# 64-byte pads between operand buffers of a two-block transformer kernel, and two weight sums that trade places

## Chip, cores, metric

The kernel runs on one core of one Trainium2 chip. The metric is device time of one execution in microseconds (us), the median over runs. Everything below is read from one profiled execution of the kernel before, and from the programs as they are built: the addresses of buffers and the order of instructions are in the built program, no time is.

## What is computed

Two transformer blocks on 512 tokens of width 1024, in float32. The reference, cut to its frame:

```python
def first_block(x, ...):
    h = rms_norm(x, norm1_w[l])
    cols = split_cols(h @ w_in[l], IN_SIZES)
    y = concatenate([short_conv_mixer(...), nsa_mixer(...), mla_mixer(...), stick_breaking_mixer(...)])
    x = x + rms_norm(y, out_norm_w) @ w_out[l]
    h2 = rms_norm(x, norm2_w[l])
    return x + square(relu(h2 @ ffn_w1[l])) @ ffn_w2[l]

def second_block(x, ...):
    h = rmsnorm(x, norm_mix_pre[l])
    proj = h @ w_in[l]
    ...
    x = x + rmsnorm(merged @ w_out[l], norm_mix_post[l])
    h = rmsnorm(x, norm_ffn_pre[l])
    f = (silu(h @ ffn_w_gate[l]) * (h @ ffn_w_up[l])) @ ffn_w_down[l]
    return x + rmsnorm(f, norm_ffn_post[l])
```

Nearly all of the work is dense products of a [512, 1024] activation (or a wider hidden one) with weight matrices.

## The kernel before

**Split products.** Every operand of a dense product is held as two float32r tiles, `hi` and `lo`, whose sum is the float32 value (`K.split`, L284 to 291: ScalarE writes `hi`, VectorE writes `lo`). A product is then three matmuls into the same PSUM bank (`K.mm3`, L317 to 321):

```python
nc.tensor.matmul(out, a[0], b[0], start=start, stop=False)
nc.tensor.matmul(out, a[0], b[1], start=False, stop=False)
nc.tensor.matmul(out, a[1], b[0], start=False, stop=stop)
```

`a` is the stationary operand (128 columns, loaded into the array by a weight load of its own for every matmul), `b` the moving one. Lines L319, L320 and L321 of the profile are these three. While matmul k streams its moving operand, the weight load of matmul k+1 reads the next stationary operand.

**Who moves and who stands.** In `tok_tile` (L486) the activation stands and the weights move, 256 columns at a time (240 or so in a few). In `fm_tile` (L503) the weights stand and the activation moves, 512 columns at a time, or 256 where only half of the tokens are there yet. In `down_tile` (L630, the second matrices of both feed-forward parts) the hidden activation stands and the weights move, 256 columns (512 for the first group of the second block). `Fast` (L510 to 607, the first matrices of both feed-forward parts) forms seven products of quarters in place of eight; weight quarters or sums of them (`a11 a12 a22 s1 s2 s3 s4`) stand, quarters of x or sums of them (`t1` to `t4`) move, 256 columns each, four mm3 a product.

**Buffers.** Tiles come from pools that are laid out in each partition one behind the other in the order in which they are opened: `cst`, `big` (one pair of activation operands), `wraw`, `wsp` (four slots each of `whi` and `wlo`, 4096 bytes), `sm` (small columns), then the pools of a phase. Almost every tile is a multiple of 128 bytes long, so the position of a buffer within 128 bytes is set by the few short tiles before it. With "half 0" for a start at a multiple of 128 and "half 64" for one that is 64 bytes behind it, the built program has: `whi`, `wlo` 0; the pair in `big` (`xh`, `xl` of both mixers, and in each feed-forward part the sums t1 to t4) 0; the first block's feed-forward operand x 64; `brh`, `brl` (the second block's branch operand, later its feed-forward operand x) 64; `hh`, `hl` (hidden activation) 64; `sah/sal` (a11, a12), `ssh/ssl` (s1, s2), `sdh/sdl` (a22) 64. The sums s3 and s4 lie in the quarter of x that no product reads, so in half 64 as well.

**Order.** The feed-forward parts interleave steps of `Fast.unit` (L577) and of the down product by a table (`merge`, PACE1 and PACE2); a scheduler then interleaves further. Everything that TensorE reads has been split by ScalarE and VectorE before.

Of the kernel before, what the change touches and what calls it, by code (L numbers as in the profile page):

```python
# [18 lines left out]
P = 128  # L19
S = 512  # L20
NT = S // P
# [32 lines left out]
# --------------------------------------------------------------------------  # L54
# host side: layout only, and constants that depend on shapes alone
# --------------------------------------------------------------------------
def _fm(w):
    """[K, n*128] -> [n, 128, K]: panels of 128 columns, all row tiles."""
    k, n = w.shape
    return np.ascontiguousarray(w.reshape(k // P, P, n // P, P).transpose(2, 1, 0, 3)).reshape(n // P, P, k)  # L60


def _kp(w, kt=4, width=256):
    """[K, n*width] -> [n * K/(128*kt), 128, kt*width]: panels of kt row tiles, the row tiles inner."""
    k, n = w.shape
    return np.ascontiguousarray(
        w.reshape(k // (P * kt), kt, P, n // width, width).transpose(3, 0, 2, 1, 4)
    ).reshape(-1, P, kt * width)
# [36 lines left out]
def prep(inp):  # L105
# [38 lines left out]
    # ---- block 2  # L144
# [74 lines left out]
# --------------------------------------------------------------------------  # L219
# device side  # L220
# --------------------------------------------------------------------------
class K:
    """Shared pools, constants and small building blocks."""

    def __init__(self, tc, a, ctx, dbg):
        self.tc, self.nc, self.a, self.dbg = tc, tc.nc, a, dbg or {}
        e = ctx.enter_context
        self.cst = e(tc.tile_pool(name="cst", bufs=1))
        self.big = e(tc.tile_pool(name="big", bufs=1))
        self.wraw = e(tc.tile_pool(name="wraw", bufs=2))  # L230
        self.wsp = e(tc.tile_pool(name="wsp", bufs=4))
        self.sm = e(tc.tile_pool(name="sm", bufs=2))
        self.dram = e(tc.tile_pool(name="dram", bufs=1, space=DRAM))
        self.ps = e(tc.tile_pool(name="ps", bufs=1, space=PSUM))
        self.n = self.flip = self.turn = self.turn2 = 0
# [6 lines left out]
        self.cols = self.cst.tile([P, a["cols"].shape[1]], F32, name="cols")  # L242

# [12 lines left out]
    def wide(self):  # L256
        """A bank for a phase of dense products alone, which has six of the eight."""
        t = WIDE[self.turn % len(WIDE)]
        self.turn += 1
        return self.psum(t)  # L260
# [13 lines left out]
    def late_dma(self, dst, src):  # L274
        """A constant of a later part: its load stays out of the way of the first ones."""
        with self.tc.issue_after(self.late.ins):
            self.nc.gpsimd.dma_start(dst, src)
# [5 lines left out]
    # hi + lo = src * scale exactly, each with 12 significant bits  # L283
# [9 lines left out]
    def copy(self, dst, src):  # L293
        """A copy out of PSUM, on ScalarE and VectorE in turn."""
# [6 lines left out]
    def weights(self, src, n, ahead=None, slot=None, parts=1):  # L301
        """One panel [128, n] from DRAM, split; slot: where it stays, if not among the others."""
# [20 lines left out]
    def spread(self, pool, out, r):  # L323
        """out[p, 128 t + i] = r[i, t]"""
# [6 lines left out]
    def mm2(self, out, a, n, hi, lo, start, stop):  # L331
        """a: hi and lo side by side, hi in the first n; out: their products one under the other."""
        steps = [(out[:n], a[:, :n], lo)]
        # the first and the last of all go to all of out
# [10 lines left out]
    def exp_ln(self, after):  # L345
        """The table set with Exp and Ln, once the activation `after` has been issued."""
# [4 lines left out]
    def rstd(self, ss, n, cnt, eps=EPS, after=None):  # L351
        """[128, n] sums of squares -> 1/sqrt(sum/cnt + eps), with one Newton step."""
# [14 lines left out]
    def junk(self):  # L367
        """Where the squares go of which only the sum is used."""
        return self.sm.tile([P, D], BF16, tag="njk", bufs=1, name=self.nm("njk"))

    def norm_table(self, pool, j, bufs=1):
        """The weight of a norm over the model width, on every partition."""
# [4 lines left out]
    def to_operand(self, op, h, t, keep=False):  # L377
        """Token-major h [128, 1024] of token tile t -> transposed, split into op; keep: also in place of h."""
# [12 lines left out]
    def norm_in(self, op, x, wt, h, t, keep=False):  # L391
        """RMS norm of token-major x [128, 1024], times wt, into the operand op; h: scratch."""
# [13 lines left out]
class Emission:  # L406
    """The parts of a phase, emitted step by step in the order of a plan."""
# [24 lines left out]
def operand(k, pool, tag):  # L432
    """A pair (hi, lo) of a whole feature-major activation."""
# [6 lines left out]
def softmax_unit(k, p, ps, bias, scale, init, acc, ssum):  # L440
    """ps: scores -> p = exp(logits - max); acc = -max, ssum = sum."""
# [5 lines left out]
def transposed(k, dst, p, n):  # L447
    """p [128 q, n keys] -> its 128-blocks transposed, [128 keys, n] in dst."""
# [7 lines left out]
def y_norm(k, y, W=256):  # L456
    """RMS-normalise token-major y [128, NT, 256] in place (weight excluded)."""
# [10 lines left out]
def heads_to_T(k, y, g, yT, w):  # L468
    """token-major y [128, NT, 256] -> transposed, weighted, split into tiles 2g, 2g + 1 of yT."""
# [9 lines left out]
def tok_tile(k, xop, t, panels, n, ps, order=range(KT)):  # L479
    """ps[128 tok, n] = x[tok tile t] @ W, W in two panels of four row tiles."""  # L480
# [15 lines left out]
def fm_tile(k, xop, w, ps, c0=0, c1=S):  # L496
    """ps[128 out features, tokens c0..c1] = W^T x, W the panel of these features."""
# [5 lines left out]
class Fast:  # L503
    """
    Products of a weight matrix with the activation x in Winograd's form of Strassen's algorithm: of the
    quarters A (the weights: output tiles by halves of the rows) and B (x: halves of the rows by halves of
    the tokens), seven products of sums in float32 instead of eight.
    """

    def __init__(self, k, x, full):  # L510
        """x: hi and lo; full(t): x of the token tile t in float32, which the sums take the place of."""
        self.k, self.x, self.full = k, x, full

    def quarter(self, i, j):
        """B of rows half i, tokens half j."""
        return [z[:, 4 * i : 4 * i + 4, 256 * j : 256 * j + 256] for z in self.x]

    def sums(self, j):
        """The sums of quarters of x, for the token tiles j and j + 2."""
# [8 lines left out]
    def split(self, t):  # L528
        """The sums, split, into t."""
# [8 lines left out]
    def weights(self, src0, src1):  # L538
        """Quarters and sums of quarters of two panels, split: by name, hi and lo, in four row tiles."""
# [3 lines left out]
        with k.tc.high_priority(AHEAD):  # L543
# [7 lines left out]
            def slot(tag, n, names):  # L551
                t = [B.tile([P, n], F32R, tag=tag + z, name=k.nm(tag + z)) for z in "hl"]
# [3 lines left out]

            k.split(*slot("sa", 1024, ("a11", "a12")), r0)
            k.split(*slot("sd", 512, ("a22",)), a22)
            slot("ss", 1024, ("s1", "s2"))
            # the quarter of x that no product takes makes room for two sums  # L560
            for i, nm in enumerate(("s3", "s4")):
                w[nm] = [z[:, 2 * i : 2 * i + 2, :].rearrange("p a (b m) -> p a b m", m=P) for z in self.quarter(0, 1)]
# [9 lines left out]
    def product(self, out, l, r):  # L572
        """out[128, 256 tokens] = quarter l of the weights, transposed, times quarter r of x."""
# [4 lines left out]
    def unit(self, src0, src1, u):  # L578
        """u[128, 2, 512] = the two output tiles of the panels src0, src1, in a step for each product."""
# [34 lines left out]
def merge(plan, **gens):  # L614
    """The steps of several generators in the order of a plan, then what is left of them."""
# [7 lines left out]
def down_tile(k, hs, t, w, kt, n, ps):  # L623
    """ps[128 tok, n] = h[tok tile t] @ W over kt tiles of hidden features."""
# [14 lines left out]
def first_block(k, xd):  # L639
    nc, tc, a = k.nc, k.tc, k.a  # L640
    xin = a["x"].rearrange("(t p) d -> p t d", p=P)
    with ExitStack() as ctx:
# [18 lines left out]
        # the norm's factor, by token: in columns, and on every partition  # L661
# [29 lines left out]
    # ---- output projection, residual; feed-forward: relu(h2 @ W1)^2 @ W2  # L691
    with ExitStack() as ctx:
# [5 lines left out]
        xop = operand(k, B, "x")  # L698

# [3 lines left out]
        def spare(z):  # L703
# [4 lines left out]
            + [spare(z) for z in ("sa", "ss")]  # L708
        )
        full = [B.tile([P, 2, D], F32, tag=z, bufs=2, name=k.nm("xf")) for z in ("hh", "hl")]  # L710
        fast = Fast(k, xop, lambda t: full[t // 2][:, t % 2, :])
        fast.pool = B
# [60 lines left out]
        for g in range(8):  # L773
            hs = pieces()
            if g == 0:
                # the first half of the tokens: the others are still on their way
# [1221 lines left out]
```

## Time and profile before

| | |
|---|---|
| runs shown | 1768.1, 1769.1, 1775.0 us; median 1769.1 |
| span of the profiled execution, first to last instruction | 1768.9 us |
| TensorE matmul busy | 1736.7 us (98%), 12,443 instructions |
| TensorE weight load busy | 1613.1 us (91%), 12,443 |
| VectorE, ScalarE, GpSimd busy | 1178.8 (67%), 878.6 (50%), 99.1 us (6%) |
| granted TensorE clock, mean | 0.993 |

No time of the profiled execution apart from its span is shown; the span is 0.2 us under the median. Matmuls are pipelined, so the busy time of one (about 280 ns for 256 columns) is longer than the distance from its start to the next one's start. That distance, called pitch below, is what sums to the span. A table of stretches counts every matmul that overlaps a stretch, so the pitch there is (length of the stretch + the time one lasts) / count.

### The profile page before, as it was taken

The numbers are of one execution on the slowest core, as the hardware profiler recorded it, in microseconds if no ns is written. First come the engines' busy times: TensorE is split into PE (matmuls) and PEld (weight loads), VectorE is DVE, ScalarE is ACT, GpSimd is POOL, SyncE is SP. The second block draws the span as 40 slices with busy tenths as digits, with TensorE's granted clock in tenths as the row PEclk, the third lists the DMA queues.
The fourth block names the chain that finished last, engine by engine and source line by source line (L and its number), as shares of the span: only waits on it lengthen the run. The fifth ranks groups of instructions, "written<-read, shape, count | busy, mean of one in ns | idle before, by whom it ended". The sixth has DMA issues, their size and how long they took to land. (4 is left out here: it accounts for less than half of the span.)

```text
span 1768.9 us, 30605 instructions
## 1 busy us (share of the span) xinstructions
PE 1736.7 (98%) x12443; PEld 1613.1 (91%) x12443; DVE 1178.8 (67%) x2194; ACT 878.6 (50%) x1625; POOL 99.1 (6%) x130
## 2 busy tenths in 40 slices
PE   8999999999999999999999999999999999999997
PEld 8888689999999998898889988889988989999997
DVE  5867855877777776987344453345436589888886
ACT  6654754553444444677324452435553565444442
POOL 0101002000000020000000000000000400000002
PEclk9999989999999999999999999999999999999999
DMA  6422104222233332121223222222235223233233
GB/s 218 159 84 71 44 1 179 84 96 97 96 107 108 104 115 97 55 90 60 84 96 108 84 69 91 97 94 72 92 100 173 90 98 118 96 108 110 94 108 108
DMA packets 50797, 174.92 MB, mean 99 GB/s; under 512 B 6075, under 2 KB 6619, under 8 KB 50656
## 3 DMA queue, kind: packets, MB, share of 16 engines
q1 hardware_dynamic: 48384, 165.38, 27.9%
q0 software_dynamic: 2272, 7.59, 1.4%
q8 instruction: 98, 1.61, 0.4%
q14 instruction: 43, 0.35, 0.1%
HBM read 166.63 MB, written 6.31 MB: 98 GB/s over the span
## 5 line engine op out<-in xcount | busy, mean ns | idle before, releaser
L288 DVE TENSOR_TENSOR wlo<-raw,whi 128x1024 fp32r<-128x1024 f32 (+2 forms) x209 | 253.5, 1214 | 188.5 <-ACT whi L287 183.0
L287 ACT ACTIVATE whi<-raw 128x1024 fp32r<-128x1024 f32 (+2 forms) x209 | 217.7, 1042 | 297.7 <-PE mm L320 167.1
L319 PE MATMUL mm<-whi,xh 128*128 128x256 f32 (+1 forms) x720 | 205.7, 287 | 7.4 <-ACT whi L287 6.6
L319 PE MATMUL mm<-xh,whi 128*128 128x512 f32 (+1 forms) x544 | 207.5, 382 | 0.6 <-DVE swv L288 0.6
L321 PE MATMUL mm<-xh,wlo 128*128 128x512 f32 (+1 forms) x544 | 206.9, 380 | 0.0
L320 PE MATMUL mm<-xl,whi 128*128 128x512 f32 (+1 forms) x544 | 206.6, 380 | 0.0
L320 PE MATMUL mm<-wlo,xh 128*128 128x256 f32 (+1 forms) x720 | 205.1, 285 | 0.0
L321 PE MATMUL mm<-whi,xl 128*128 128x256 f32 (+1 forms) x720 | 204.6, 285 | 0.0
L319 PEld LDWEIGHTS mm<-whi,xh 128*128 128x128 f32 x720 | 138.0, 192 | 9.1 <-ACT whi L287 6.6
L320 PEld LDWEIGHTS mm<-wlo,xh 128*128 128x128 f32 x720 | 138.1, 192 | 1.7 <-issue 0.9
L321 PEld LDWEIGHTS mm<-whi,xl 128*128 128x128 f32 x720 | 137.9, 192 | 1.1 <-issue 0.9
L319 PE MATMUL mm<-whi,hh 128*128 128x256 f32 (+1 forms) x428 | 119.2, 280 | 0.4 <-ACT hh L287 0.4
L320 PE MATMUL mm<-wlo,hh 128*128 128x256 f32 (+1 forms) x428 | 119.5, 279 | 0.0
L321 PE MATMUL mm<-whi,hl 128*128 128x256 f32 (+1 forms) x428 | 119.3, 279 | 0.0
L319 PEld LDWEIGHTS mm<-xh,whi 128*128 128x128 f32 x544 | 102.3, 188 | 18.4 <-DVE swv L288 0.8
L321 PEld LDWEIGHTS mm<-xh,wlo 128*128 128x128 f32 x544 | 102.4, 188 | 18.0
L320 PEld LDWEIGHTS mm<-xl,whi 128*128 128x128 f32 x544 | 102.4, 188 | 17.3
L319 PE MATMUL mm<-brh,whi 128*128 128x512 f32 (+1 forms) x224 | 84.9, 380 | 0.2 <-ACT brh L287 0.2
L320 PE MATMUL mm<-brl,whi 128*128 128x512 f32 (+1 forms) x224 | 84.4, 377 | 0.7 <-DVE brl L288 0.7
L321 PE MATMUL mm<-brh,wlo 128*128 128x512 f32 (+1 forms) x224 | 84.8, 379 | 0.0
L319 PEld LDWEIGHTS mm<-whi,hh 128*128 128x128 f32 x428 | 80.4, 188 | 0.8 <-ACT hh L287 0.6
L320 PEld LDWEIGHTS mm<-wlo,hh 128*128 128x128 f32 x428 | 80.5, 188 | 0.2
(797 smaller groups left out, 5026.3 us busy)
## 6 DMA issues: line engine op xcount, KB each, us to landing
raw<-in_f_dram SPq DMA_DIRECT2D x50, 512.0 KB, 3.5
raw<-in_gates_dram SPq DMA_DIRECT2D x24, 512.0 KB, 3.4
raw<-in_wb_dram SPq DMA_DIRECT2D x24, 512.0 KB, 3.5
raw<-in_fd_dram SPq DMA_DIRECT2D x22, 512.0 KB, 4.1
raw<-in_wo_dram SPq DMA_DIRECT2D x16, 512.0 KB, 4.1
raw<-in_rvg_dram SPq DMA_DIRECT2D x16, 512.0 KB, 3.4
raw<-in_gvg_dram SPq DMA_DIRECT2D x16, 512.0 KB, 3.4
sraw<-in_f_dram SPq DMA_DIRECT2D x14, 512.0 KB, 3.8
```

Of the source, the lines that this page charges most:

```text
L287: nc.scalar.activation(hi, src, AF.Copy)
L288: nc.vector.tensor_tensor(lo, src, hi.bitcast(F32), ALU.subtract)
L319: nc.tensor.matmul(out, a[0], b[0], start=start, stop=False)
L320: nc.tensor.matmul(out, a[0], b[1], start=False, stop=False)
L321: nc.tensor.matmul(out, a[1], b[0], start=False, stop=stop)
```

## The change

Seven tiles of 64 bytes (`pad`, 128 partitions x 16 floats) are put between other tiles, each with a memset on GpSimd. In `Fast.weights` a22 takes the place of s4 in the unused quarter of x, s4 takes a22's place in `sd`, and `ss` may come from a pool of its own that follows the phase's pool. The diff without the lines that only drop comments:

```diff
@@ class K, __init__
         self.wraw = e(tc.tile_pool(name="wraw", bufs=2))
+        self.shift(e(tc.tile_pool(name="wpad", bufs=1)))
         self.wsp = e(tc.tile_pool(name="wsp", bufs=4))
         self.sm = e(tc.tile_pool(name="sm", bufs=2))
+        self.shift(e(tc.tile_pool(name="spad", bufs=1)))
...
+    def shift(self, pool):
+        self.nc.gpsimd.memset(pool.tile([P, 16], F32, name=self.nm("pad")), 0.0)
@@ class Fast, weights
             def slot(tag, n, names):
-                t = [B.tile([P, n], F32R, tag=tag + z, name=k.nm(tag + z)) for z in "hl"]
+                pool = self.spool if tag == "ss" else B
+                t = [pool.tile([P, n], F32R, tag=tag + z, name=k.nm(tag + z)) for z in "hl"]
...
+            for i, nm in enumerate(("a22", "s3")):
+                w[nm] = [z[:, 2 * i : 2 * i + 2, :].rearrange("p a (b m) -> p a b m", m=P) for z in self.quarter(0, 1)]
             k.split(*slot("sa", 1024, ("a11", "a12")), r0)
-            k.split(*slot("sd", 512, ("a22",)), a22)
+            k.split(*w["a22"], a22.rearrange("p (a b m) -> p a b m", a=2, m=P))
             slot("ss", 1024, ("s1", "s2"))
-            for i, nm in enumerate(("s3", "s4")):
-                w[nm] = [z[:, 2 * i : 2 * i + 2, :].rearrange("p a (b m) -> p a b m", m=P) for z in self.quarter(0, 1)]
+            slot("sd", 512, ("s4",))
@@ first_block, feed-forward
         xop = operand(k, B, "x")
+        k.shift(B)
...
-            + [spare(z) for z in ("sa", "ss")]
+            + [spare("sa"), k.shift(B) or spare("ss")]
         )
+        k.shift(B)
         full = [B.tile([P, 2, D], F32, tag=z, bufs=2, name=k.nm("xf")) for z in ("hh", "hl")]
-        fast.pool = B
+        fast.pool = fast.spool = B
@@ second_block, feed-forward
-        fast.pool = B
+        fast.pool, fast.spool = B, ctx.enter_context(tc.tile_pool(name="ffn2s", bufs=1))
         wt = k.norm_table(B, 5)
         fo = B.tile([P, NT, D], F32, name="fo")
+        k.shift(B)
+        k.shift(fast.spool)
```

In the built program `whi`, `wlo` go from half 0 to half 64, `hh`, `hl`, `sah/sal`, `sdh/sdl` from 64 to 0; `ssh/ssl`, the operands x of the feed-forward parts and the pair in `big` stay. Counted over all float32r matmuls in their order, by the half in which the moving operand starts and the half in which the stationary operand of the next matmul starts (some 200 with another position are left out):

| columns, halves (moving, next stationary) | before | with the change |
|---|---|---|
| 256, (0, 0) | 2,819 | 710 |
| 256, (64, 64) | 1,319 | 536 |
| 256, (0, 64) | 4,030 | 1,610 |
| 256, (64, 0) | 566 | 5,879 |
| 512, (0, 0) | 1,419 | 76 |
| 512, (64, 64) | 0 | 570 |
| 512, (0, 64) | 58 | 1,343 |
| 512, (64, 0) | 568 | 56 |

With the change, about 300 of the equal pairs of 256 columns stand alone, at a switch between two kinds of product.

Instructions keep their number and, on TensorE, their place; names change. TensorE in the second block's feed-forward part, behind a piece of the down product, where a product of the unit in work begins (`mm_17737`; its operands are the moving `brh/brl`, and s4). Before:

```order
L320 MATMUL mm_17937<-wlo_17767,hh_16921 128x256
L319 MATMUL mm_17737<-brh_13910 128x256
L320 MATMUL mm_17737<-brl_13911,brh_13910 128x256
L321 MATMUL mm_17737<-brh_13910,brl_13911 128x256
L319 MATMUL mm_17737<-brh_13910 128x256
```

And with the change:

```order
L327 MATMUL mm_17960<-wlo_17796,hh_16944 128x256
L326 MATMUL mm_17760<-brh_13926,sdh_17693 128x256
L327 MATMUL mm_17760<-brl_13927,sdh_17693 128x256
L328 MATMUL mm_17760<-brh_13926,sdl_17694 128x256
L326 MATMUL mm_17760<-brh_13926,sdh_17693 128x256
```

The matmuls are the same; s4 is read from `sd` where it was read from `br`. ScalarE in the same part, the `hi` halves of one unit's weights (`sd` was a22, the `br` rows s3 and s4; the other rows of the stretch belong to the down product). Before:

```order
L287 ACTIVATE sdh_16372<-sraw_16365 128x512
...
L287 ACTIVATE ssh_16376<-sraw_16365 128x512
L287 ACTIVATE sah_16368<-raw_16364 128x1024
L287 ACTIVATE brh_13910<-sraw_16365 128x2x256
L287 ACTIVATE ssh_16376<-sraw_16365 128x512
L1950 ACTIVATE u_16189<-u_16189 128x1024
L287 ACTIVATE brh_13910<-raw_16364 128x2x256
```

And with the change (`sd` is s4, the `br` rows a22 and s3):

```order
L294 ACTIVATE brh_13926<-sraw_16388 128x2x256
...
L294 ACTIVATE ssh_16397<-sraw_16388 128x512
L294 ACTIVATE sah_16391<-raw_16387 128x1024
L294 ACTIVATE brh_13926<-sraw_16388 128x2x256
L294 ACTIVATE ssh_16397<-sraw_16388 128x512
L1963 ACTIVATE u_16212<-u_16212 128x1024
L294 ACTIVATE sdh_16399<-raw_16387 128x512
```

The six pieces have the same sizes and stand in the same order.

## Rows read from the trace of the kernel before

**Rows 1.** The page's busy times by engine.

```profile
PE 1736.7 (98%) x12443; PEld 1613.1 (91%) x12443; DVE 1178.8 (67%) x2194; ACT 878.6 (50%) x1625; POOL 99.1 (6%) x130
```

**Rows 2.** Stages: stretch, length, busy (instructions) by engine, PEclk, DMA share, GB/s.

```profile
357.60:626.40 268.80, 268.80 (x2343) 268.79 (x2342) 204.77 (x319) 125.65 (x162) 0.00 (x0) 1.00 0.31 103
...
1437.60:1731.50 293.90, 292.67 (x2479) 289.98 (x2478) 248.26 (x409) 131.91 (x188) 0.00 (x0) 1.00 0.34 112
1731.50:1768.90 37.40, 24.72 (x218) 24.52 (x216) 24.09 (x44) 12.09 (x31) 12.12 (x10) 0.90 0.28 85
```

**Rows 3.** The same table, stretches of 256-column matmuls of one kind alone.

```profile
674.00:687.00 13.00, 13.00 (x110) 13.00 (x110) 6.12 (x8) 4.20 (x6) 0.00 (x0) 1.00 0.19 58
...
606.00:608.60 2.60, 2.60 (x24) 2.60 (x23) 2.44 (x4) 2.10 (x3) 0.00 (x0) 1.00 0.00 2
549.50:563.00 13.50, 13.50 (x121) 13.50 (x120) 8.12 (x15) 2.82 (x4) 0.00 (x0) 1.00 0.47 152
...
336.00:357.00 21.00, 21.00 (x181) 21.00 (x180) 12.00 (x17) 4.87 (x7) 0.00 (x0) 1.00 0.32 101
321.20:334.80 13.60, 13.60 (x122) 13.60 (x122) 13.22 (x20) 10.19 (x16) 0.00 (x0) 1.00 0.22 72
1428.50:1437.50 9.00, 9.00 (x79) 9.00 (x78) 7.25 (x10) 6.34 (x8) 0.58 (x1) 1.00 0.21 66
```

**Rows 4.** TensorE in order of time, feed-forward of block one: start, length, instruction.

```profile
374.52 0.28 PE L319 MATMUL mm<-xh,sah 128*128 128x256 f32 x1
...
375.94 0.29 PE L319 MATMUL mm<-xh,ssh 128*128 128x256 f32 x1
...
377.32 0.28 PE L319 MATMUL mm<-xh,sah 128*128 128x256 f32 x1
```

**Rows 5.** TensorE in order of time, two breaks by transposes (L385).

```profile
318.01 0.60 PE L385 MATMUL tp<-ident,xf 128*128 128x128 f32 x4
...
318.57 0.28 PE L321 MATMUL mm<-xh,wlo 128*128 128x256 f32 x1
...
319.98 0.28 PE L321 MATMUL mm<-xh,wlo 128*128 128x256 f32 x1
...
320.45 0.60 PE L385 MATMUL tp<-ident,xf 128*128 128x128 f32 x4
```

**Rows 6.** TensorE in order of time, where both operands change halves.

```profile
335.06 0.28 PE L321 MATMUL av<-xh,wlo 128*128 128x256 f32 x1
335.18 0.28 PE L319 MATMUL mm<-whi,hh 128*128 128x256 f32 x1
335.30 0.28 PE L320 MATMUL mm<-wlo,hh 128*128 128x256 f32 x1
335.42 0.28 PE L321 MATMUL mm<-whi,hl 128*128 128x256 f32 x1
```

**Rows 7.** TensorE in order of time, 512 columns: first and last of three runs.

```profile
665.33 0.39 PE L321 MATMUL mm<-xh,wlo 128*128 128x512 f32 x1
...
673.49 0.39 PE L321 MATMUL mm<-xh,wlo 128*128 128x512 f32 x1
...
884.15 0.39 PE L319 MATMUL mm<-brh,whi 128*128 128x512 f32 x1
...
888.73 0.39 PE L321 MATMUL mm<-brh,wlo 128*128 128x512 f32 x1
...
1098.82 0.40 PE L321 MATMUL mm<-brh,wlo 128*128 128x512 f32 x1
...
1103.72 0.40 PE L321 MATMUL mm<-brh,wlo 128*128 128x512 f32 x1
```

**Rows 8.** Groups by line and shape: count, then busy us, mean ns, idle before.

```profile
L319 PE MATMUL mm<-whi,xh 128*128 128x256 f32 x688 | 196.8, 287 | 7.4 <-ACT whi L287 6.6 <-ACT xh L290 0.7
...
L320 PE MATMUL mm<-wlo,hh 128*128 128x256 f32 x420 | 116.3, 277 | 0.0
```

More of the change, by code (lines that the diff above doesn't have):

```diff
@@ L226, in __init__ @@
         self.tc, self.nc, self.a, self.dbg = tc, tc.nc, a, dbg or {}
+        self.n = self.flip = self.turn = self.turn2 = 0
         e = ctx.enter_context
@@ L230, in __init__ @@
         self.wraw = e(tc.tile_pool(name="wraw", bufs=2))
+        self.shift(e(tc.tile_pool(name="wpad", bufs=1)))
         self.wsp = e(tc.tile_pool(name="wsp", bufs=4))
         self.sm = e(tc.tile_pool(name="sm", bufs=2))
+        self.shift(e(tc.tile_pool(name="spad", bufs=1)))
         self.dram = e(tc.tile_pool(name="dram", bufs=1, space=DRAM))
         self.ps = e(tc.tile_pool(name="ps", bufs=1, space=PSUM))
-        self.n = self.flip = self.turn = self.turn2 = 0
         self.mixed = False
```

## The prediction

> **What bounds the kernel now.** I read the busy line of the page first [rows 1]: matmuls cover 98% of the span, VectorE 67%, ScalarE 50%, GpSimd 6%. The stage table then shows the two feed-forward loops, 268.80 and 293.90 us, in which TensorE idles for 0.00 and 1.23 us at a full granted clock [rows 2]. So TensorE's own pace sets the time, and the change leaves its instructions and their order alone. What is left to it is the pitch of one matmul against the next, and that is not one number. Stretches of the same work, three matmuls of 256 columns a product, differ [rows 3]; with the 0.28 us of the last one added to each length:
>
> - moving operand and next stationary operand in equal halves: 13.28/110 = 120.7 ns for (0, 0) at 674 us, 2.88/24 = 120.0 for (64, 64) at 606 us. One matmul more or less at the edges shifts the first by 1%, so I take 120.0 for both.
> - opposite halves: 13.78/121 = 113.9 for (0, 64) at 549 us and 13.88/122 = 113.8 for (64, 0) at 321 us, but 21.28/181 = 117.6 for (0, 64) at 336 us and 9.28/79 = 117.5 for (64, 0) at 1,428 us. All six stretches have a granted clock of 1.00, which is the upper of the two levels (2.4 GHz), and TensorE idles in none.
>
> So opposite halves have two paces, called **fast** (113.8) and **middle** (117.6) here, and both sign pairs show both. At 512 columns the order is turned round [rows 7]: equal halves (0, 0) take (673.49 - 665.33)/36 = 226.7 ns, opposite ones (884.15 to 888.73 over 20) 229.0 or (1,098.82 to 1,103.72 over 21) 233.3. The groups agree with the first finding from another side: the mean of one matmul is 287 ns where whi and xh, both in half 0, meet, and 277 where wlo and hh, in opposite halves, do [rows 8].
>
> **What picks the pace** is how a run begins. Behind the first of two transposes, twelve matmuls from 318.57 to 319.98 us go at 117.5 ns, behind the second, with the same operands, the next 122 go fast [rows 5, 3]. At 335.18 us moving and stationary operand both change halves with one equal pair between, and the run behind it, entered from a fast one, stays at 117.6 for its whole stretch [rows 6, 3]. Inside the feed-forward loop, by contrast, twelve equal pairs (1.42/12 = 118.3 ns) stand between two fast runs of (0, 64), and the next twelve are at 115.0 with the settling in it [rows 4]: a long run of equal pairs seems to hand over in the fast pace, a single one does not always.
>
> **The change, part by part.** Counts are of the built programs; prices are [rows 3] unless said.
>
> *Token-tile products of the mixers and both projections:* some 2,230 matmuls of 256 columns (whi, wlo moving, half 0 to 64) go from equal to (64, 0). All fast they give 2,230 x 6.2 = -13.8 us, all middle 2,230 x 2.4 = -5.4. They are broken up by transposes and element-wise waits, and behind a break both paces occur [rows 5], so I take the middle between them, **-9.6**.
>
> *Feed-forward loops:* 4,767 matmuls of 256 columns. Their time now is 268.80 + 293.90 - 1.23 idle - 11.0 (48 matmuls of 512 columns by [rows 7]) = 550.5 us [rows 2], or 115.5 each: a quarter (1,226) equal, the rest mostly fast. With the change nearly all are opposite, but half of them (64, 0), and where the work passes between kinds of product both operands flip, which leaves a lone equal pair, as at 335.18 us [rows 6]. All fast: 4,767 x 113.8 = 542.5. All middle: 560.6. Some 300 lone pairs at 120 in place of either add 1.9 or 0.7. So -6.1 to +10.8. The nearest rows for the entry are split (rows 4 fast, rows 6 middle), so I take half and half: 551.5 + 1.3, **+2.3**. This is the term on which the sign hangs.
>
> *512 columns:* 1,343 pairs go from (0, 0) to (0, 64), 570 from (64, 0) to (64, 64). With 226.7 for equal and 229.0 for opposite [rows 7]: +3.1 - 1.3 = **+1.8**. If the new opposite ones are at 233.3 it is +8.9 - 1.3 = +7.6; if the ones removed are half at 233.3 and the new ones at 229.0, +0.5.
>
> *Losers:* the same pads make equal pairs of some that are opposite now: 174 at 305 to 328 us, where the stretch at 321 us is fast, 185 at 1,405 to 1,431 us, where the one at 1,428 us is middle, and 135 of the first output projection, which I take as middle too. 174 x 6.2 + 320 x 2.4 = **+1.8**; all of them fast now, it would be +3.1.
>
> *Last stage,* from 1,731.5 us: 24.72 us for 218 matmuls, 113.4 each, all (0, 64) and fast [rows 2]. They become (64, 0): nothing if fast, 209 x 3.8 = 0.8 if middle; I take **+0.4**.
>
> *Pads and swapped sums:* seven memsets on GpSimd, which works for 99.1 us in 130 instructions, 0.76 each [rows 1]: 5.3 us on an engine with nothing to do in either loop [rows 2], and no one reads a pad. If that cover were gone, a memset would hold up TensorE only where it delayed a tile's first writer. a22 and s4 have the same size, the same writers and the same place in ScalarE's order, and the pools keep their number of buffers, so no wait is added: **0** for both.
>
> Sum: -9.6 + 2.3 + 1.8 + 1.8 + 0.4 = -3.3, so 1,765.6 from the profiled span of 1,768.9, and 0.2 more against the median of the runs, 1,769.1. I predict **1,765.5**. A measurement of this kernel can tell about 0.5%, 8.8 us, from no change; by that bound this is no change.
>
> The row that speaks for the change is the 120.0 of equal against 113.8 of opposite halves at the same clock and with no idle time [rows 3]. The Trainium skill, "TensorE: Matmul & The Clock Gate", in its step-by-step part, step 1, says against it: "Loading the next tile's weights doesn't steal SBUF read bandwidth from the running matmul." By that sentence the halves would not matter and the sum would be 0; the trace disagrees, by 6.2 ns in 120.
>
> **Rivals.**
>
> *1. Every opposite pair runs fast.* For it: in the loops nearly all opposite pairs are fast now (115.5 on average with a quarter equal [rows 2], 113.9 at 549 us [rows 3]). Against it: rows 5 and 6. It gives -13.8 - 6.1 + 1.8 + 1.8 + 0 - 0.8 (the 191 at 336 us become fast too) = -17.1, so 1,752; with the 512 columns at their lower end, 1,750.7.
>
> *2. The middle pace takes the loops, and it is slower.* Today the loops owe their fast pace to long runs of equal pairs that reset it [rows 4]; the change removes these and puts a flip of both operands in their place, the one form of entry that rows 6 show going into the middle pace. Then -5.4 + 10.8 + 1.8 + 1.8 + 0.8 = +9.8, so 1,779, and with 512 columns at 233.3 (+7.6 for +1.8) 1,784.7. From all fast to all middle the time rises by 26.9 us; so it is slower by over 8.8 us once less than 4% of the pairs are fast with 512 columns at 229.0, or less than a quarter at 233.3.
>
> *3. Halves are not the cause,* but go along with it: which product, which buffer. For it: only one place in the trace shows the same product in both paces [rows 5]. Against it: all equal stretches are at 120, four places with other operands and stages are not [rows 3]. It gives 1,769. The sentence of the Trainium skill above stands on this side.
>
> **How the numbers follow.** Rows 4 and 6 are one against one for the loops; forecast (a mixture) 0.47, rival 1 0.33, rival 2 0.15, rival 3 0.05. Forecast and rival 3 lie within 0.5%, rival 1 beyond it on the fast side, rival 2 at 1,779 and over on the slow side: faster 0.33, same 0.52, slower 0.15. The range goes from just under rival 1 with 512 columns at their lower end, 1,749, to rival 2 with 512 columns about a third of the way to their upper end, 1,781.
>
> **What would show it.** Right: pure stretches of whi against xh fall from 120 to 113.8 or 117.6, with the mean of that group falling from 287 [rows 8]; 512-column runs of xh at 229 or more; the lengths of the two loops add up to about 565. Rival 1 shows loops of 557 together, rival 2 of 573. Wrong altogether would be equal pairs at less than 120 or opposite ones at 120, a third pace, or idle time of TensorE in the loops, which would mean that something other than the pads moved.

## The result, and the profile after

The change makes the kernel slower: 1,786.0 us median (1,782.6 to 1,789.0, 4 runs) against 1,768.6 (1,766.1 to 1,775.0, 4 runs). The ratio, of the means, is 1.0092, with a 95% interval of 1.007 to 1.0114. The profiled execution spans 1,783.8 us. The prediction was 1,765.5, no change, in a range of 1,749 to 1,781; it was wrong. Two executions of some 4,406 us, one of run f2 below and one of the kernel before, are in no ratio of this text.

The busy line of the page, with the change, answers to [rows 1]:

```profile
PE 1752.6 (98%) x12443; PEld 1622.1 (91%) x12443; DVE 1176.9 (66%) x2194; ACT 879.8 (49%) x1625; POOL 98.2 (6%) x137
```

The same 12,443 matmuls take 15.9 us more, and no other engine moves by more than 2 us. The stage table with the change has the two feed-forward loops, the last stage (the columns are those of [rows 2]), and, second, 4,095 matmuls of the second block's mixers:

```profile
362.60:635.90 273.30, 273.30 (x2343) 273.30 (x2342) 205.15 (x319) 125.91 (x163) 0.00 (x0) 1.00 0.30 101
683.80:1375.10 691.30, 690.51 (x4095) 604.30 (x4094) 373.42 (x726) 342.10 (x647) 17.26 (x43) 1.00 0.28 91
1449.40:1746.20 296.80, 295.25 (x2480) 292.80 (x2479) 248.41 (x409) 132.09 (x188) 0.00 (x0) 1.00 0.34 110
1746.20:1783.80 37.60, 25.56 (x218) 25.35 (x216) 24.14 (x44) 12.09 (x31) 12.14 (x10) 0.89 0.27 85
```

The mixers' stage of the kernel before:

```profile
673.90:1362.80 688.90, 688.12 (x4096) 608.12 (x4096) 373.30 (x726) 341.71 (x646) 17.89 (x43) 1.00 0.28 91
```

Loops +4.5 and +2.9 us, mixers +2.4, last stage's matmuls +0.8, at a granted clock that is the same to 0.01. TensorE idles for 0.3 us more in the second loop (1.55 for 1.23) and for no more than 0.01 us more in the other three stages. The pitch did it. The matmuls of the six stretches of [rows 3], with the change:

```profile
683.90:696.60 12.70, 12.70 (x110) 12.70 (x109) 6.09 (x8) 4.12 (x6) 0.00 (x0) 1.00 0.18 56
615.10:617.60 2.50, 2.50 (x24) 2.50 (x23) 2.50 (x5) 2.11 (x3) 0.00 (x0) 1.00 0.00 0
557.40:571.20 13.80, 13.80 (x121) 13.80 (x120) 7.92 (x14) 2.76 (x3) 0.00 (x0) 1.00 0.42 147
340.90:362.00 21.10, 21.10 (x182) 21.10 (x181) 13.19 (x20) 5.42 (x8) 0.00 (x0) 1.00 0.29 100
325.50:339.70 14.20, 14.20 (x122) 14.20 (x121) 13.17 (x19) 10.16 (x17) 0.00 (x0) 1.00 0.22 73
1440.30:1449.30 9.00, 9.00 (x78) 9.00 (x77) 7.21 (x10) 6.31 (x8) 0.74 (x3) 1.00 0.22 70
```

The first, equal pairs that were at 120, is at 12.98/110 = 118.0. The third, a stretch of the loop that ran fast, is at 14.08/121 = 116.4. The fifth, one of the losers, is at 14.48/122 = 118.7: its pairs are equal now, and equal pairs below 120 were on the prediction's list of what would show it wrong altogether. Where the pieces of the loop change over [rows 4], the run that began behind long equal pairs at 115.0 ns now goes at (382.14 - 380.73)/12 = 117.5:

```profile
379.31 0.28 PE L326 MATMUL mm<-xh,sah 128*128 128x256 f32 x1
...
380.73 0.28 PE L326 MATMUL mm<-xh,ssh 128*128 128x256 f32 x1
...
382.14 0.29 PE L326 MATMUL mm<-xh,sah 128*128 128x256 f32 x1
```

And the 36 matmuls of 512 columns that took 226.7 ns [rows 7] take (683.30 - 674.90)/36 = 233.3:

```profile
674.90 0.39 PE L328 MATMUL mm<-xh,wlo 128*128 128x512 f32 x1
...
683.30 0.39 PE L328 MATMUL mm<-xh,wlo 128*128 128x512 f32 x1
```

Both programs issue the same matmuls in the same order (some 70 between 313 and 350 us stand a few places apart), so nearly every pitch can be set against its twin. The addresses come from the built programs. Summed by what happened to the pair, in us: token products -4.5, loops +7.2, 512 columns +7.8, losers +1.3, last stage +0.9, which makes +12.7. Another 3.5 lie in the first block's attention, on matmuls that are no split products (last section).

### The profile page after: what moved, and what is told of

It is laid out like the page before. It is cut to its first block, busy times and chain, and to the rows that moved or that the text cites. A ratio compares the mean times of both kernels' runs of the same rounds, so it can differ in the third digit from the quotient of the medians.

```text
span 1783.8 us, 30614 instructions
## 1 busy us (share of the span) xinstructions
PE 1752.6 (98%) x12443; PEld 1622.1 (91%) x12443; DVE 1176.9 (66%) x2194; ACT 879.8 (49%) x1625; POOL 98.2 (6%) x137
```

## The experiments

The first theory was the prediction's own, with its second rival as the outcome: halves of 128 bytes and the way a run begins. The rival was that something else that the change does costs the time. Here **distance** is the start of the moving operand less that of the next stationary one, modulo 256 bytes, so 0, 64, 128 or 192. By halves, 0 and 128 are equal pairs, 64 and 192 opposite ones. Distance was not part of the first theory; the first four runs brought it up. A **lone** equal pair is one with opposite pairs on both sides.

**Pads of 128 bytes** (e1), the change otherwise whole:

```diff
-        self.nc.gpsimd.memset(pool.tile([P, 16], F32, name=self.nm("pad")), 0.0)
+        self.nc.gpsimd.memset(pool.tile([P, 32], F32, name=self.nm("pad")), 0.0)
```

> All of the change, but each pad is 128 bytes in place of 64: the swapped sums, the extra pool and the seven memsets stay, and every operand of a split product has the half that it had before. If the halves are the cause, this is the kernel before: 1,768 to 1,770 us (ratio 1.000), loops together about 563 us, 512-column stretches of xh at 227 ns. If the pads, the pool of its own or the swapped sums cost the time, it is 1,784 to 1,788 (ratio 1.009).

Measured: ratio 1.0066 (1.0042 to 1.009). The halves are those of the kernel before, and most of the loss is there. The loops take 572.7 us together, where 563 was expected:

```profile
363.20:636.70 273.50, 273.50 (x2342) 273.50 (x2342) 205.56 (x319) 125.99 (x163) 0.00 (x0) 1.00 0.31 101
1451.50:1750.70 299.20, 297.32 (x2480) 294.62 (x2479) 248.52 (x410) 132.40 (x189) 0.00 (x0) 0.99 0.34 110
```

The 512-column stretch takes (683.96 - 675.56)/36 = 233.3 ns, as with the change:

```profile
675.56 0.39 PE L328 MATMUL mm<-xh,wlo 128*128 128x512 f32 x1
...
683.96 0.39 PE L328 MATMUL mm<-xh,wlo 128*128 128x512 f32 x1
```

So the half of 128 bytes is not the whole of it: either the address matters in a coarser unit, or the rival holds.

**One kind of product at a time** (e2, e3, e4). Each slot of `whi` and `wlo` is 64 bytes longer and its contents begin 0 or 64 bytes in, so that each use can have its own half; `SLOT` is a list of which slot the scheduler gives. e2 and e3 start from the kernel before, e4 has the change's feed-forward layout without the first two pads:

```diff
-                hi = self.wsp.tile([P, 1024], F32R, tag="hi", name=self.nm("whi"))
+                o = 16 * (half ^ int(SLOT[self.wn]))
+                self.wn += 1
+                hi = self.wsp.tile([P, 1040], F32R, tag="hi", name=self.nm("whi"))[:, o : o + 1024]
...
-    return [k.weights(src[i], n) for i in range(2)]
+    return [k.weights(src[i], n, half=half) for i in range(2)]
...
-        fm_tile(k, xop, k.weights(a["wF3"][m], 1024), ps)
+        fm_tile(k, xop, k.weights(a["wF3"][m], 1024, half=1), ps)
```

The second pair of lines is one of e2's uses, the third one of e3's; e4 has `half=1` in the feed-forward parts' uses alone. To make room, a small tile (`ss32`, 128 bytes) has one buffer in place of two in these three runs, and in g1 and h2 below.

> The kernel before, with whi and wlo in half 64 only where they move in 256 columns past a mixer's or a projection's activation; 2,261 pairs go from (0, 0) to (64, 0), all others stay. By halves and entry: these go at the middle pace, since they begin behind breaks and lone pairs, some 117.5 ns for 119.8, so -4 to -6 us: 1,763 to 1,765. If such runs could begin fast: -14, 1,755. If halves don't matter: 1,769.

> The kernel before, with whi and wlo in half 64 only where they stand and xh moves in 512 columns; 1,330 pairs go from (0, 0) to (0, 64), all others of 256 columns but 128 stay. By halves: 228.4 to 233.2 ns each, +6 us: 1,775. By the price that I had put on it before (229.0): +2 to +3, 1,771. If it is TensorE's clock that took the time of this stage: no change in the stretches.

> The feed-forward parts of the change alone: their pads, the swapped sums, whi and wlo in half 64 there; the mixers and the projections keep the halves they had. By halves and entry: the loops lose the long runs of equal pairs that hand over in the fast pace, three in four lone pairs lead into the middle pace, so the loops take 7 us more (570) and the last stage 1 more: 1,777 to 1,778. If the loops' loss came from what happens in the mixers before them: 1,769 to 1,771.

Measured: e2 1.0062 (1.004 to 1.0085), e3 1.0101 (1.0074 to 1.0128), e4 1.0045 (1.0028 to 1.0062). e4 agrees with its expectation in the loops, 569.5 us, and in the whole, some 8 us more; but its mixers' stage, whose halves were left alone, takes 691.5 us, 2.6 more than before, so the whole agrees in part by luck. e2 and e3 do not agree: their loops, in which no half was changed, take 14.7 and 16.8 us more than before (2.7 of e3's are idle time). e2's loops:

```profile
360.80:636.40 275.60, 275.60 (x2343) 275.60 (x2342) 206.04 (x319) 125.89 (x163) 0.00 (x0) 1.00 0.31 100
1445.80:1747.70 301.90, 300.09 (x2480) 297.57 (x2479) 248.73 (x410) 132.43 (x189) 0.00 (x0) 0.99 0.33 109
```

Slots of 4,160 bytes keep the halves where I wanted them, but the slots then start at all four places within 256 bytes, and the buffers behind them move too, so these runs do not price one product alone. In both runs' loops some 2,580 pairs of 256 columns go from distance 192 to 64, with every long run of equal pairs still in place; in e2 these pairs take 10.2 of the 14.7 us.

The runs also gave variety. The mean pitch in ns by distance, from ten profiles (before, the change, e1 to e4, and f1 to f4 below), disturbed pitches over 140 ns at 256 columns and 260 at 512 left out:

| distance | 512 columns | 256 columns |
|---|---|---|
| 0 | 228.5 | 119.2 |
| 64 | 229.8 | 117.4 |
| 128 | 232.4 | 118.7 |
| 192 | 233.1 | 115.0 (fast and middle mixed) |

By halves of 128 bytes, 0 and 128 are the same, and so are 64 and 192; at 512 columns they are 4 and 3 ns apart, and the kernel before had its xh at distance 0, the best one. That is the second theory: the distance sets the pitch.

**Pads of 256 bytes** (f1): the change whole, all distances as before. Its second pad is left out, since 256 bytes need no correction.

```diff
-        self.shift(e(tc.tile_pool(name="spad", bufs=1)))
-        self.nc.gpsimd.memset(pool.tile([P, 16], F32, name=self.nm("pad")), 0.0)
+        self.nc.gpsimd.memset(pool.tile([P, 64], F32, name=self.nm("pad")), 0.0)
```

> All of the change with pads of 256 bytes (the second pad of the constant pools left out, which 256 bytes don't need): swapped sums, own pool and memsets stay, every distance between a moving operand and the next stationary one is what it was, counted in 256 bytes. New theory, distance in 256 bytes: as the kernel before, ratio 1.000 (0.997 to 1.003), 512-column pairs of xh at 228 ns, loops at 563 us. Rival, the pads, pool or swapped sums: ratio 1.007 and more, as with pads of 128 bytes.

**The first pad 192 bytes** (f2), all halves of 128 bytes as in the change:

```diff
-        self.shift(e(tc.tile_pool(name="wpad", bufs=1)))
+        self.shift(e(tc.tile_pool(name="wpad", bufs=1)), 48)
...
-    def shift(self, pool):
+    def shift(self, pool, n=16):
...
```

> The change with the pad ahead of whi and wlo 192 bytes long in place of 64: all halves of 128 bytes are those of the change, but xh is 64 bytes behind whi, counted in 256 bytes, and not 192. Distance theory: 512-column pairs of xh go from 233.2 to 230.1 ns, -4 us against the change, the 256-column ones of the mixers (distance 192 in place of 64) at 117.5 or less, and the down products likewise: 1,777 to 1,781 where the kernel before has 1,769, ratio 1.005 to 1.007. By halves of 128 bytes alone: as the change, 1.009.

**The mixers' activation 64 bytes later** (f3), the kernel before otherwise:

```diff
+def big_operand(k, later):
+    hi = k.big.tile([P, KT * S + 16], F32R, tag="xh", name=k.nm("xh"))
+    lo = k.big.tile([P, KT * S + 48], F32R, tag="xl", name=k.nm("xl"))
+    oh, ol = (16, 0) if later else (0, 48)
...
-        xop = operand(k, k.big, "x")
+        xop = big_operand(k, 1)
```

> The kernel before with the mixers' activation (and that of the second projection) 64 bytes later, weights, feed-forward parts and the rest where they were. 2,243 pairs of 256 columns go from distance 0 to 192, 1,386 of 512 columns from 0 to 64. Distance theory: 256 columns from 119.4 to 116 or 117.6 (-4 to -7 us), 512 columns from 228.3 to 230.1 (+2.5): ratio 0.997 to 0.999. By halves alone with the prices of the change: -4.4 and +6.5, 1.001.

Measured: f1 0.9995 (0.9979 to 1.0011), f2 1.0004 (0.9991 to 1.0017), f3 0.9946 (0.9925 to 0.9967). The mixers' stage, with pads of 256 bytes, with the first pad at 192, and with the activation 64 bytes later, one profile each:

```profile
670.10:1358.90 688.80, 688.01 (x4095) 608.10 (x4094) 373.26 (x726) 341.77 (x646) 17.85 (x43) 1.00 0.29 91
```

```profile
673.40:1356.70 683.30, 682.51 (x4096) 600.43 (x4095) 373.10 (x726) 341.94 (x647) 17.78 (x43) 1.00 0.29 92
```

```profile
675.10:1357.80 682.70, 681.91 (x4096) 601.18 (x4096) 373.15 (x726) 341.80 (x647) 17.76 (x43) 1.00 0.29 92
```

f1 settles the rival: with six of the seven memsets, the swapped sums and the pool of its own there, the time is that of before. f2 has every half that the change has and is 8.0 us shorter than the change in this stage, by 128 more bytes at one place. It does not come from its loops, which take 573.2 us together, 3.1 more than with the change:

```profile
351.80:625.80 274.00, 274.00 (x2341) 274.00 (x2341) 204.88 (x319) 125.89 (x163) 0.00 (x0) 1.00 0.31 101
1430.20:1729.40 299.20, 297.02 (x2480) 294.28 (x2479) 248.73 (x409) 132.33 (x188) 0.00 (x0) 0.99 0.34 110
```

Its 512-column stretch goes from 664.73 to 672.97 us, 228.9 a matmul:

```profile
664.73 0.39 PE L328 MATMUL mm<-xh,wlo 128*128 128x512 f32 x1
...
672.97 0.39 PE L328 MATMUL mm<-xh,wlo 128*128 128x512 f32 x1
```

f3 shows the way round that helps: moving weights 64 bytes ahead of the activation (distance 192 at 256 columns, 64 at 512). The stage is 6.2 us shorter than before, and the ratio lower than the expected 0.997 to 0.999. f2 too did better than its expectation of 1.005 to 1.007; I had counted the token products' gain from 64 to 192 too low.

**Loops of one kind of pair** (f4): the quarters of x lie one behind the other, so that the moving ones start in half 0 and the unused one, which holds two sums, in half 64. The kernel before otherwise.

```diff
+    return Quarters(h, 0, 1072), Quarters(l, 3088, 0)
...
-        xop = operand(k, B, "x")
+        xop = x_operand(k, B, "x")
```

> The kernel before with the feed-forward operand x moved so that every moving operand of the loops lies in half 0 and every stationary one in half 64, all at distance 192: no pair in the loops is equal, and none flips. If the fast pace needs only that it is not disturbed: loops at 113.8 ns, -7 us, ratio 0.996 to 0.997 (the first pieces lose 1 to 2). If the long runs of equal pairs are what hands over in the fast pace, the loops fall into the middle one and stay there: up to +9 us, ratio 1.005.

**One product turned over** (g2): the same with s4 and its quarter of x in the other halves, so that two lone equal pairs stand in each unit.

```diff
-    return Quarters(h, 0, 1072), Quarters(l, 3088, 0)
+    return Quarters(h, 2096, 0, 3120, 1024), Quarters(l, 0, 3088, 1024, 2064)
...
-            for i, nm in enumerate(("s3", "s4")):
+            for i, nm in enumerate(("a22", "s3")):
```

> The single-kind loops with one product of the seven turned over: its moving quarter of x in half 64, its stationary sum s4 in half 0 (and a22 in the unused quarter, as in the change), distance 64, so that two lone equal pairs stand around its 12 matmuls in each unit. If lone equal pairs throw the loops out of the fast pace: most runs behind them in the middle one, loops 565 to 570 us in place of the 556 of the single-kind loops. If only the turned product itself has another pace: 12 matmuls in some 134 at up to 4 ns more, loops at 558.

**One equal run a unit** (h1): x as in g2, the sums where the kernel before has them, so s4's 12 matmuls are equal pairs. Against f4:

```diff
-    return Quarters(h, 0, 1072), Quarters(l, 3088, 0)
+    return Quarters(h, 2096, 0, 3120, 1024), Quarters(l, 0, 3088, 1024, 2064)
```

> The single-kind loops with the last but one product of a unit (s4) at distance 0: its quarter of x in half 64 again, so that each unit holds one run of 12 equal pairs, 410 in all. If a long equal run hands over in the fast pace every time: loops at 542.5 + 410 x 6.2 ns + 12 = 557 to 559 us in every execution, runs closer together than the single-kind loops' (1,763 to 1,787), median 4 below the kernel before, ratio 0.997 to 0.998. If equal runs do nothing for the pace: spread as wide as without them and 2.5 us more, ratio 1.001.

Measured: f4 1.0001 (0.9974 to 1.0028), g2 1.0028 (1.001 to 1.0046), h1 0.9992 (0.9977 to 1.0006). The two loops, f4 first, then g2, then h1:

```profile
358.00:624.50 266.50, 266.48 (x2342) 266.17 (x2341) 204.15 (x319) 125.54 (x162) 0.00 (x0) 1.00 0.32 104
...
1434.90:1724.10 289.20, 287.75 (x2479) 285.11 (x2478) 247.20 (x409) 131.39 (x188) 0.00 (x0) 1.00 0.35 113
```

```profile
353.00:624.70 271.70, 271.70 (x2343) 271.65 (x2343) 205.17 (x319) 125.74 (x163) 0.00 (x0) 1.00 0.31 102
...
1435.70:1731.00 295.30, 293.55 (x2479) 291.00 (x2479) 248.29 (x409) 131.66 (x188) 0.00 (x0) 1.00 0.34 111
```

```profile
358.70:625.70 267.00, 267.00 (x2342) 266.68 (x2341) 204.69 (x319) 125.75 (x162) 0.00 (x0) 1.00 0.32 103
...
1436.00:1728.40 292.40, 290.40 (x2480) 287.83 (x2479) 248.20 (x409) 131.98 (x188) 0.00 (x0) 0.99 0.35 112
```

Together 555.7, 567.0 and 559.4 us (562.7 before, 570.1 with the change). f4's loops are as its first outcome has them, 7.0 us shorter than before, but over 12 executions between 1,763 and 1,787 us its ratio shows no gain. h1's loops come out near the expected 557 to 559, its ratio does not (0.997 to 0.998 was expected), and its 12 times are closer together, 1,763 to 1,772.

Turning over one product in seven costs 11.3 us, where its own 374 pairs at 4 ns each would come to 1.5. Set against f4, 10.2 of these lie on 4,324 pairs that stay at distance 192. What it does to the runs behind it is plain in g2's trace, two runs of the same operands and 206 and 208 pairs, each behind a lone equal pair:

```profile
386.10:410.30 24.20, 24.20 (x208) 24.20 (x207) 19.20 (x30) 10.85 (x13) 0.00 (x0) 1.00 0.34 115
411.90:435.40 23.50, 23.50 (x210) 23.50 (x209) 18.72 (x29) 9.48 (x13) 0.00 (x0) 1.00 0.33 113
```

(24.20 + 0.28)/208 = 117.7 and (23.50 + 0.28)/210 = 113.2: one middle, one fast, and each keeps its pace to the end. Counted over runs of six pairs or more behind a lone equal pair: 31 fast and 39 middle in g2, 58 and 148 with the change. Behind equal runs of four or more at distance 0, runs at distance 192 are fast: 90 fast and 1 middle in the kernel before, 39 and 0 in h1. Runs at distance 64 are not: 1 fast and 140 middle in e2 and e3 together.

So for runs at distance 192, lone equal pairs are what throws them out of the fast pace, and a long equal run puts them back. The change does a second thing to its loops: 2,572 of their pairs go from distance 192 to 64, and these take 7.6 us more (114.0 to 116.9 ns), while 738 that stay at 192 take 1.7 more, and 1,154 equal pairs that become opposite give 2.6 back. No run of this case separates these two for the change's own loops.

What comes behind a lone pair at distance 0 hangs on the pace before it, as the same traces show. A run at distance 64 keeps that pace (33 of 34 in g2, 51 of 51 with the change). A run at 192 that comes from a fast one is middle (14 of 15, and 13 of 13); from a middle one it is fast in 15 of 21 and 13 of 22. What decides in this last case stays open.

**Both moves** (g1: f3 and f4, and the second block's branch operand at distance 0), and **all three** (h2: g1 with the equal run of h1). Against f4, and against g1:

```diff
+    z = pool.tile([P, 2 * KT * S + 32], F32R, tag="br", name=k.nm("br"))
+    return z[:, 16 : 16 + 2 * KT * S], z
...
-        xop = operand(k, k.big, "x")
+        xop = big_operand(k, 1)
```

```diff
-    return Quarters(z, 6176, 16), Quarters(z, 7200, 3088)
+    return Quarters(z, 16, 6176, 1040, 4128), Quarters(z, 2064, 7200, 3088, 5152)
```

> The kernel before with both moves that helped: mixers' activation 64 bytes later, and the feed-forward operand x laid out so that the loops hold one kind of pair (distance 192); besides, the second block's branch operand, 512 columns, goes from distance 64 to 0. If the gains add: -7 of the mixers, -7 of the loops, -1 of the branch operand: ratio 0.990 to 0.992. If the loops' fast pace hangs on what runs before them: ratio 0.995.

> That, with the mixers' activation 64 bytes later and the branch operand at distance 0. If gains add and the pace is handed over every time: -4 in the loops, -7.5 in the mixers, -1 of the branch operand, ratio 0.992 to 0.994, with a spread as that of the kernel before. Otherwise as the two moves together without the equal run, 0.995 with a spread of 20 us.

Measured: g1 0.995 (0.9922 to 0.9979), h2 0.994 (0.9917 to 0.9963), 1,760.2 us median beside 1,770.2 of the kernel before. The gains of the mixers and the loops are both in g1's and h2's traces (mixers 682.7 and 683.1, loops 555.5 and 558.7 together); the branch operand gave nothing that shows. g1's ratio is nevertheless the 0.995 of its second outcome, not 0.990 to 0.992; its 12 times lie between 1,753 and 1,775, h2's six between 1,755 and 1,761. h2 beats both kernels; that it beats f3 (0.9946) is not shown.

**The same kernels once more** (i1 and i2: f4; i3: the change; i4: h1), for other executions of them:

> The single-kind loops once more, for another execution of theirs: its times lay between 1,763 and 1,787 us, and its one profile is of the fastest. If the pace a loop is entered with stays, an execution above 1,770 has a loop, or long parts of one, at 117.6 ns, loops together at 565 to 574 us; one near 1,763 has 556. If the spread comes from TensorE's clock in the first stage: loops at 556 in any case.

> The single-kind loops a third time, the same two outcomes: loops at 565 to 574 us in an execution above 1,770 if the pace of entry stays, at 556 in any case if the spread is the clock of the first stage.

> The change once more. If the middle pace of its loops is the rule behind lone equal pairs: loops at 568 to 572 us again, about a quarter of the entries fast, 512-column pairs of xh at 233 ns, and what differs from the first execution lies in the stretch at 200 to 265 us and at the first weights of the second loop.

> The loops with one equal run of 12 a unit once more: loops at 557 to 560 us again, every run behind the equal ones fast.

Measured, one execution each: 1,767.5, 1,760.6, 1,782.2 and 1,762.8 us, beside 1,766.9 of the kernel before. The loops take 557.8 and 555.9 us in i1 and i2, 570.7 in i3 (the entries behind lone pairs are 57 fast and 149 middle) and 560.4 in i4, just over the 557 to 560 expected. So the change's loops repeat. No execution of f4 that was profiled has a loop in the middle pace; what made some of its times as long as 1,787 stays open, and the guess that such a loop keeps a bad entry is not shown.

## Why the prediction was wrong

*That the pitch is all* was right: instruction order, other engines, pads and swapped sums cost nothing (f1, 0.9995), and the loops idle for only 0.3 us more than before. Three terms of the sum failed, and with them the sum: -3.3 stood there, +12.7 was measured on the same pairs.

*The unit of the 512-column term was wrong* (+1.8, measured +7.8). I sorted operands by halves of 128 bytes, because the kernel before has almost only distances 0, 64 and 192 (3,889, 566 and 4,030 of its pairs of 256 columns, 249 at 128) and no row of it told 0 from 128. The term failed by it: I priced the new opposite pairs at 229.0, the lower of two rows, and the pairs that become equal at 226.7. Both rows were of the branch operand at distance 64 [rows 7]; the change puts xh at 192, where nearly every pair takes 233, and the branch operand at 128, about 232. The dearer case that I gave, +7.6, is near the measured sum by luck: its parts were +8.9 and -1.3, measured +6.7 and +1.1.

*The loops,* half fast and half middle, +2.3: measured +7.2. The step that failed is that the next run is as often fast as middle: 28% of the entries behind lone pairs are fast. The second rival's mechanism, that lone flips replace the runs that reset the pace, is shown for runs at distance 192 (f4, g2, h1). It is not the whole: most of the loss lies on the pairs that go to distance 64, which are middle even behind long equal runs (e2, e3). Of the two rows that I weighed, the both-sided flip at 335.18 us [rows 6] was the one that resembles the change's entries, and it pointed to the middle pace: a fast run, a lone equal pair, and a run at distance 192, the case that is middle in 14 of 15.

*The token products,* -9.6: measured -4.5. The step that failed is the middle between the two paces: they go to distance 64 for the most part, and their mean is 117.4 ns. Losers (+1.8, measured +1.3) and last stage (+0.4, +0.9) had the right size.

The second rival with its dearer 512 columns stood at 1,784.7; the span was 1,783.8. That it is so near is in part luck: its loops, +10.8, were 3.6 too dear, and 3.5 us of the span lie in the attention. It had 15%, since I let the fast loops of the trace of before count for the loops of the change, although the change takes away the runs that they owed their pace to.

The sentence of the Trainium skill, "TensorE: Matmul & The Clock Gate", step 1 of its step-by-step part, that weight loading takes nothing from the running matmul, would have made pads free. The runs disagree where the length of the pads differs (and one pad is left out): 233.3 against 226.7 ns for the 36 matmuls of 512 columns, with pads of 128 and of 256 bytes (the latter from 661.50 to 669.66 us):

```profile
661.50 0.39 PE L327 MATMUL mm<-xh,wlo 128*128 128x512 f32 x1
...
669.66 0.39 PE L327 MATMUL mm<-xh,wlo 128*128 128x512 f32 x1
```

## What to carry to other kernels

Where TensorE has no idle time left and every matmul loads new weights, look at where the moving operand and the next stationary one start, and sort by the whole address before believing in a unit: a control that moves things by the unit you believe in (pads of 128 bytes here) costs one run and would have ended the first theory at once. Do not average the two paces of a loop that can keep either; ask what sets the pace at each entry, and whether the change leaves that in place. A layout that is best for one shape can be worst for another (distance 192 at 256 and at 512 columns), so price shapes apart.

## What was not expected of the hardware

The starts of the operands matter modulo 256 bytes (pads of 256 cost nothing, 0.9995, pads of 128 cost 0.7%): with 512 columns 228.5, 229.8, 232.4 and 233.1 ns a matmul at distances 0, 64, 128 and 192, disturbed pitches left out (the mixers' stage, where 1,690 of some 2,080 lie, has a granted clock of 1.00). Opposite halves have two paces at 256 columns (113.2 and 117.7 in g2), which stay for some 200 matmuls there and are chosen at the entry. What in TensorE makes the starts matter, no run here shows.

Executions of one kernel differ by some 10 us, and part of it is TensorE's granted clock in the first block's attention. The stretches 200 to 240 and 240 to 265 us, the kernel before, the change, and the change once more:

```profile
200.00:240.00 40.00, 36.65 (x174) 26.64 (x174) 25.44 (x54) 26.50 (x49) 0.00 (x0) 0.79 0.00 1
240.00:265.00 25.00, 24.06 (x204) 22.64 (x203) 17.76 (x49) 15.20 (x47) 0.00 (x0) 1.00 0.00 1
```

```profile
200.00:240.00 40.00, 36.65 (x188) 27.32 (x187) 26.51 (x61) 27.15 (x51) 0.00 (x0) 0.83 0.00 1
240.00:265.00 25.00, 23.56 (x161) 22.39 (x160) 15.48 (x39) 11.29 (x32) 0.00 (x0) 0.80 0.00 1
```

```profile
200.00:240.00 40.00, 36.72 (x214) 27.55 (x213) 30.77 (x68) 28.44 (x56) 0.00 (x0) 0.91 0.00 1
240.00:265.00 25.00, 23.64 (x176) 22.68 (x176) 14.11 (x41) 15.07 (x46) 0.00 (x0) 0.86 0.00 1
```

TensorE idles for over 3 us in the first of them and runs part of the time at the lower of its two levels (1.2 GHz), a different part in each execution. The 3.5 us that the first profile of the change has more in that stage are not in the second one, so they are no part of what the change does. A second place is the start of the second loop, where the first weights are split: the idle time ahead of one matmul was 0.78 us in the kernel before and 3.32 in f3, and the 512-column matmuls behind the longer one followed each other at 425 ns, in a stretch (1,436.80 to 1,440.30 us) with a granted clock of 0.67:

```profile
1437.03 0.38 PE L319 MATMUL mm<-xh,sdh 128*128 128x256 f32 x1 [3.32 <-ACT sdh L287]
...
1438.57 0.63 PE L320 MATMUL mm<-wlo,hh 128*128 128x512 f32 x1
1438.99 0.63 PE L319 MATMUL av<-whi,hh 128*128 128x512 f32 x1
1439.42 0.63 PE L320 MATMUL av<-wlo,hh 128*128 128x512 f32 x1
```
